# Where the silu gate is multiplied in, and who adds the keys' sums, in a one-core encoder step

## Chip, cores and metric

One Trainium2 chip, one of its cores. The time is that of one execution on the device in microseconds, the median of the runs. The core has TensorE (PE; its weight loads are listed apart as PEld), VectorE (DVE), ScalarE (ACT), GpSimd (POOL) and SyncE (SP), which here only issues DMAs. Each engine works through its own instructions in order; semaphores let one wait for another or for a DMA to land.

## What is computed

One layer of a streaming encoder for 1024 prompt tokens and 64 tokens of a running stream with 512 cached ones, all in fp32. A combined projection feeds two groups of heads; group A is latent attention, group B gated linear attention. What bears on the change:

```python
# group A, keys
kv = (latent @ w_ukv).reshape(B, S, MLA_HEADS, QK_NOPE + V_DIM)
k_nope, v = kv[..., :QK_NOPE], kv[..., QK_NOPE:]
k = jnp.concatenate([k_nope, jnp.broadcast_to(krope[:, :, None, :], ...)], axis=-1)
k = rms_norm(k, g_k_head)            # mean over all 192 columns of a head
# group B, output
o = rms_norm(o, g_gla_out.reshape(GLA_HEADS, GLA_DV))
b_out = o.reshape(B, T, GLA_WIDTH) * jax.nn.silu(r)
# both
x = x + gate1 * (jnp.concatenate([a_out, b_out], axis=-1) @ w_out)
h2 = rms_norm(x, g_norm2) * (1 + scale2) + shift2
x = x + gate2 * (jnp.square(jax.nn.relu(h2 @ w_up)) @ w_down)
```

## The kernel before

A large matmul is made of three fp32r products (high by high, high by low, low by high parts; `mm3`, lines 94 to 96 of the helper). Who makes the parts is `split`: ScalarE copies the high part (line 102), VectorE subtracts (line 103). The work is written as generators, "streams", that a small planner interleaves by estimated times; below that, the framework's scheduler sets each engine's order, except where an instruction is pinned. The order is fixed before the kernel runs: an instruction that waits holds up all behind it on its engine, and SP's queue holds up the DMAs behind it.

The stages the change touches, in order of time:

**Query latents (about 262 to 345 us).** PE makes the latents' rows tile by tile (D1), the columns of the three query groups Q0 to Q2, and the keys and values of the cached tokens. Each latent tile goes PE, ScalarE (square and sum, line 699), GpSimd (`rstd`, lines 121 and 122), VectorE (cn, line 701), PE (transposes of cn, line 715), ScalarE (cl, line 718), then a DMA to lat_d. Beside this `gates()` (line 1371) takes r, the raw gate of group B (128 x 4 heads x 1088 tokens in DRAM, r_d), in four chunks of 272 tokens: load, Silu on ScalarE, store back to r_d. Its tiles live in the pool qp, r with two buffers.

**Keys (`keys_values`, line 986; from 262 to about 456 us).** For each tile of 128 keys, two head pairs each: PE makes k and v in one PSUM bank (g); VectorE copies kn (line 996); ScalarE squares and sums each head (line 998) into ss; VectorE copies v (line 999); GpSimd adds the rotary part's sum ksum and 192 * EPS (line 1000) and takes the power -0.5 (line 1002); VectorE multiplies kn by it (line 1007) and krt (line 1008); PE transposes kn (line 1014) and krt (line 1021). ksum comes from `rotate` (line 966), once for up to four tiles.

**Attention (345 to 545 us), with `out_early` (line 1280) at its end.** While the last attention units run, mh and ml, the parts of mix for the first 272 tokens, are made: group A's heads times rs_d (the softmax sums' reciprocals, broadcast), group B's heads times r, then `split`; PE then does the first four of eight blocks of the projection between the last attention steps.

**Output projection (545 to 640 us, `main` at line 1440).** Four rounds w = 0 to 3 of 272 tokens each. For each later round the half mx[0] (group A) is multiplied by mb (from rs_d), the half mx[1] (group B) by mr (from r_d), both by `gate` (line 1278), then split. Each block of 128 output columns is 24 matmuls; VectorE adds the residual (line 1501), SP stores x2 (line 1503). `load_gates` (line 1452) issues mb (line 1458, one buffer) and mr (line 1459), `load_mix` (1443) mx, `load_x` (1461) the residual. `norm2` follows each round: PE sums squares (line 1523), VectorE (1526) and GpSimd (1527) make the factor st, VectorE a diagonal dg (1530), PE broadcasts it (1534).

Of the kernel before, what the change touches and what calls it, by code (L numbers as in the profile page):

```python
# [10 lines left out]
F32 = mybir.dt.float32  # L11
F32R = mybir.dt.float32r
I32 = mybir.dt.int32
AF = mybir.ActivationFunctionType
ALU = mybir.AluOpType
# [4 lines left out]
P = 128  # L20
# [6 lines left out]
H = 4  # L27
FF = 4096
EPS = 1e-6
# [3 lines left out]
HT = TOK // 2  # L33
# [39 lines left out]
def layer(ctx: ExitStack, tc: tile.TileContext, I, O):  # L73
    nc = tc.nc
    ACT, DVE, POOL, PE, SP = nc.scalar, nc.vector, nc.gpsimd, nc.tensor, nc.sync
# [39 lines left out]
    mhalf = const.tile([P, 4], F32, name="mhalf")  # L115
# [10 lines left out]
    pin = tc.keep_in_program_order  # L126
# [840 lines left out]
    def rotate(k, kn, tab, n):  # L967

        x, cs, sn = kraw[:n, k:k + kn], tabk[:n, tab:tab + kn, 0], tabk[:n, tab:tab + kn, 1]
        a, t = (kw.tile([P, 4, 64], F32, name=name, bufs=1)[:n, 0:kn] for name in ("ra", "rt"))  # L970
        ACT.activation(a, x, AF.Square)
        DVE.reduce_sum(ksum[:n, k:k + kn], a, axis=AX.X)
        DVE.tensor_tensor(out=a, in0=x, in1=cs, op=ALU.mult)
        DVE.tensor_tensor(out=t, in0=x, in1=sn, op=ALU.mult)
        DVE.tensor_tensor(out=x[:, :, 0:32], in0=a[:, :, 0:32], in1=t[:, :, 32:64], op=ALU.subtract)
        DVE.tensor_tensor(out=x[:, :, 32:64], in0=a[:, :, 32:64], in1=t[:, :, 0:32], op=ALU.add)
# [7 lines left out]
    def keys_values(lh, ll, ki, n, kv, slot, ahead=4500):  # L984
        ukh, ukl = groups["UK"]
        kn = kw.tile([P, H, P], F32, name="kn")
        ss = kw.tile([P, 8], F32, name="ssk")

        kr = kw.tile([P, 2, P], F32, name="krt", bufs=1)
        for g in range(2):  # L990
            pk = g_bank()
            for kt in range(2):
                mm3(pk[:n], lh[:, kt, :n], ll[:, kt, :n], ukh[:, kt, 512 * g:512 * g + 512],
                    ukl[:, kt, 512 * g:512 * g + 512], kt == 0, kt == 1)
            pg = pk[:n].rearrange("p (h c) -> p h c", h=2)
            DVE.tensor_copy(kn[:n, 2 * g:2 * g + 2], pg[:, :, 0:P])
            for j in range(2):
                ACT.activation(kr[:n, j], pg[:, j, 0:P], AF.Square, accum_out=ss[:n, 2 * g + j:2 * g + j + 1])
            DVE.tensor_copy(kv.v[:n, slot, 2 * g:2 * g + 2], pg[:, :, P:2 * P])
            POOL.tensor_scalar(out=ss[:n, 4 + 2 * g:6 + 2 * g], in0=ss[:n, 2 * g:2 * g + 2], scalar1=ksum[:n, ki:ki + 1],  # L1000
                               scalar2=192 * EPS, op0=ALU.add, op1=ALU.add)
            POOL.tensor_tensor(out=ss[:n, 4 + 2 * g:6 + 2 * g], in0=ss[:n, 4 + 2 * g:6 + 2 * g], in1=mhalf[:n, 0:2], op=ALU.pow)
            yield 1300, 0, None

        rs = [ss[:n, a:a + 2].rearrange("p (h o) -> p h o", o=1).broadcast_to([n, 2, P]) for a in (4, 6)]
        for g in range(2):
            DVE.tensor_tensor(out=kn[:n, 2 * g:2 * g + 2], in0=kn[:n, 2 * g:2 * g + 2], in1=rs[g], op=ALU.mult)
        DVE.tensor_tensor(out=kr[:n].rearrange("p g (e c) -> p (g e) c", e=2), in0=kraw[:n, ki:ki + 1].broadcast_to([n, H, 64]),
                          in1=ss[:n, 4:8].rearrange("p (h o) -> p h o", o=1).broadcast_to([n, H, 64]), op=ALU.mult)
        cs = slice(P * slot, P * slot + n)  # L1010
        yield 0, ahead, None
        tp = heads(tp_bank())
        for hd in range(H):
            PE.transpose(tp[:, hd, :n], kn[:n, hd], ident[:n, :n])
        ACT.activation(kv.kh[:, :, cs], tp[:, :, :n], AF.Copy, scale=gkhT)
        DVE.scalar_tensor_tensor(out=kv.kl[:, :, cs], in0=tp[:, :, :n], scalar=gkhT, in1=f32(kv.kh[:, :, cs]),
                                 op0=ALU.mult, op1=ALU.subtract)
        yield 450, 800, None
        tp = heads(tp_bank())
        for g in range(2):  # L1020
            PE.transpose(tp[:, g, :n], kr[:n, g], ident[:n, :n])
        for e in range(2):
            hi, lo = slice(64 * e, 64 * e + 64), slice(64 - 64 * e, P - 64 * e)
            ACT.copy(kv.kr[hi, e::2, cs], tp[hi, 0:2, :n])
            DVE.tensor_tensor(out=kv.kr[lo, e::2, cs], in0=tp[hi, 0:2, :n], in1=f32(kv.kr[hi, e::2, cs]), op=ALU.subtract)
        yield 450, 600, None
# [244 lines left out]
    HW = HT // 2  # L1271
# [5 lines left out]
    def gate(t, r):  # L1277
        return DVE.tensor_tensor(out=t, in0=t, in1=r, op=ALU.mult)

    def sums_row(k, kn, t0, n):  # L1280
        return rs_d[k:k + kn, t0:t0 + n].rearrange("(o h) t -> o h t", o=1).broadcast_to([P, kn, n])

    def out_early():
        yield 1000, 0, has("wo 4")
        mixh.append(wctx.enter_context(tc.tile_pool(reuse_waits="tile", name="mixh", bufs=1, side="right")))
        mh, ml = mix_pair()
        b3 = mixh[0].tile([P, 1, HW], F32, name="b3")
        mixh.append((mh, ml))
        def fetch(src, k, kn, t=None):
            t = rawp.tile([P, kn, HW], F32, name="raw") if t is None else t  # L1290
            SP.dma_start(t, sums_row(k, kn, 0, HW) if src is rs_d else src[:, k:k + kn, 0:HW])
            return t

        def halves(k, kn, t):
            split(mh[:, k:k + kn], ml[:, k:k + kn], t, DVE)

        b0, t0, t1 = fetch(rs_d, 0, 3), fetch(mix_d, 0, 3), fetch(mix_d, 4, 2)
        fetch(rs_d, 3, 1, b3)
        yield 0, 5000, None
        pin(gate(t0, b0))  # L1300
        halves(0, 3, t0)
        r1, t3 = fetch(r_d, 0, 2), fetch(mix_d, 3, 1)
        yield 0, 2500, None
        pin(gate(t1, r1))
        halves(4, 2, t1)
        t2, r2 = fetch(mix_d, 6, 2), fetch(r_d, 2, 2)
        pin(gate(t3, b3))
        halves(3, 1, t3)
        yield 0, 3000, None
        pin(gate(t2, r2))  # L1310
        halves(6, 2, t2)
        yield 0, 4250, lambda: not units
        for m in range(4):
            yield 0, 0, lambda: state["banks"] < 4
            state["banks"] += 1
            po = mm_bank()[:, 0:HW]
            for kt in range(KT):
                n, o = wo_place(m, kt)
                mm3(po, wo[n][0][:, o], wo[n][1][:, o], mh[:, kt], ml[:, kt], kt == 0, kt == KT - 1)
                yield 340, 600, None  # L1320
            early.append(po)
# [49 lines left out]
    def gates():  # L1371

        yield 0, 0, has("k 8", "end C1")
        for c in range(4):
            r = qp.tile([P, 4, HT // 2], F32, name="r", bufs=2)
            ts = slice(c * HT // 2, (c + 1) * HT // 2)
            SP.dma_start(r, r_d[:, :, ts])
            yield 0, 3500, None
            ACT.activation(r, r, AF.Silu)
            SP.dma_start(r_d[:, :, ts], r)  # L1380
            yield 0, 1000, None
        tc.keep_in_program_order(ACT.preload_act_table_set("natural_log_exp_and_others"))

# [42 lines left out]
    with ExitStack() as octx:  # L1426
# [11 lines left out]
            return X[10 * (h + 1) + 1 + k // 4][:, k % 4, hs]  # L1438

        def main():  # L1440
            ld = {}

            def load_mix(w):
                if w >= 4:
# [4 lines left out]
                    for _, t0, n, o in place(c)[2]:  # L1449
                        SP.dma_start(ld[c][b][:, :, o:o + n], mix_d[:, 4 * b:4 * b + 4, t0:t0 + n])  # L1450

            def load_gates(w):
                if w >= 4:
                    return
                c = WORDER[w]
                ld[c] += [xw.tile([P, 4, HW], F32, name="mr", bufs=2), xw.tile([P, 4, HW], F32, name="mb", bufs=1)]
                for _, t0, n, o in place(c)[2]:
                    SP.dma_start(ld[c][3][:, :, o:o + n], sums_row(0, H, t0, n))
                    SP.dma_start(ld[c][2][:, :, o:o + n], r_d[:, :, t0:t0 + n])

            def load_x(w):
                if w >= 4:
# [8 lines left out]
            for w, c in enumerate(WORDER):  # L1471
                _, _, parts = place(c)
                if w == 0:
                    mh, ml = mixh[1]
                else:
                    mx = ld.pop(c)
                    mh, ml = mix_pair() if w == 2 else [xw.tile([P, 8, HW], F32R, name=f"m{x}1", bufs=1) for x in "hl"]
                    gate(mx[0], mx[3])
                    split(mh[:, 0:4], ml[:, 0:4], mx[0], DVE)
                    gate(mx[1], mx[2])  # L1480
                    split(mh[:, 4:8], ml[:, 4:8], mx[1], DVE)
                if w == 0:
                    load_x(0)
                    load_mix(1)
                load_gates(w + 1)
                load_x(w + 1)
                load_mix(w + 2)
                acc = last[:, 0:HW] if w == 3 else nw.tile([P, HW], F32, name="acc")
                for m in range(8):
# [586 lines left out]
```

## Time and profile before

| what | value |
|---|---|
| median of 3 runs | 1329.35 us (1327.03 to 1332.3) |
| the profiled execution's own time | 1331.06 us |
| its span, first to last instruction | 1329.2 us |
| granted TensorE clock, mean | 0.999 |
| DMA | 191.40 MB, mean 144 GB/s |

The profile gives each engine's busy time; PE's matmuls are pipelined and their ends modelled, so the number of matmuls in a stretch tells more than its busy share. A row of a timeline has start, duration, engine, line, operation, out<-in, shapes and count; brackets at its end give the idle time of the engine just before and what ended it. A row of the waits has total, times and longest. ACTIVATION_READ_ACCUMULATOR is the second half of an activation that also sums. SPq and ACTq are DMA issues.

### The profile page before, as it was taken

Reading aid. Unit: us, or ns where it says so; the run is one execution under the profiler, and the core shown is the slowest. Engines: PE = TensorE matmul, PEld = TensorE weight load, DVE = VectorE, ACT = ScalarE, POOL = GpSimd, SP = SyncE. Lnnn points to the kernel's source line nnn. Section 1 sums busy time; section 2 is a strip of 40 time slices with the busy share of each in tenths; the row PEclk is TensorE's granted clock in tenths of the full one; section 3 lists DMA queues with packets and bytes.
Section 4 is the critical chain, followed back from the end, with each engine's and each line's share of the span. In section 5 each row is a group of like instructions: output and inputs, shape, how many; then the busy total and the mean of one; then the engine's idle time right before and its main releaser. Section 6 shows DMA issues by size and latency. Waiting matters only on the chain.

```text
span 1329.2 us, 25834 instructions
## 1 busy us (share of the span) xinstructions
PE 1307.7 (98%) x9925; PEld 1248.1 (94%) x9925; DVE 911.7 (69%) x2032; ACT 647.2 (49%) x1608; POOL 77.7 (6%) x136
## 2 busy tenths in 40 slices
PE   9999999999999999999999999999999999999999
PEld 8899999889777889999999999999999999999998
DVE  4898787466577767576999976566546955864554
ACT  5375554564266666443765445444444343333332
POOL 0100010121112200001000000000000000000000
PEclk9999999999999999999999999999999999999999
DMA  9420123384445202792346654344259645442441
GB/s 344 147 75 1 49 77 89 97 238 128 158 131 155 74 16 81 203 283 86 99 150 210 196 172 157 124 158 140 86 206 384 223 160 193 161 127 85 135 127 35
DMA packets 164653, 191.40 MB, mean 144 GB/s; under 512 B 15686, under 2 KB 116914, under 8 KB 164402
## 3 DMA queue, kind: packets, MB, share of 16 engines
q1 hardware_dynamic: 162002, 186.46, 44.3%
q10 hardware_dynamic: 2528, 3.29, 0.7%
q8 instruction: 78, 1.28, 0.4%
q14 instruction: 45, 0.37, 0.1%
HBM read 136.22 MB, written 53.49 MB: 143 GB/s over the span
## 4 chain that ended last, share of the span: by engine, by line
PE 73%; DVE 11%; DMA 7%; ACT 5%; issue 2%; POOL 2%; SPq 0%; ACTq 0%; DVEq 0%; POOLq 0%
PE mm L94 13%; PE mm L96 12%; PE mm L95 12%; PE g L94 5%; PE g L96 5%; PE g L95 5%; PE tp L94 3%; PE tp L96 3%; PE tp L95 3%; PE mm L1094 3%; PE g L1124 2%; PE g L886 1%; PE mm L179 1%; DMA mb<-rs_d 1%; PE tp L1134 1%
## 5 line engine op out<-in xcount | busy, mean ns | idle before, releaser
L102 ACT CAST opers<-quad 128x512 fp32r<-128x512 f32 x112 | 69.5, 621 | 183.3 <-PE mm L96 147.0
L103 DVE TENSOR_TENSOR opers<-quad,opers 128x512 fp32r<-128x512 f32 x112 | 77.3, 690 | 113.7 <-ACT opers L102 113.7
L96 PE MATMUL mm<-opers 128*128 128x272 f32 x448 | 128.7, 288 | 0.0
L94 PE MATMUL mm<-opers 128*128 128x272 f32 x448 | 128.4, 287 | 0.3 <-DVE e L2003 0.3
L95 PE MATMUL mm<-opers 128*128 128x272 f32 x448 | 128.2, 286 | 0.0
L94 PE MATMUL mm<-ah,wh 128*128 128x272 f32 x424 | 121.8, 288 | 0.0
L96 PE MATMUL mm<-ah,wl 128*128 128x272 f32 x424 | 121.8, 288 | 0.0
L95 PE MATMUL mm<-al,wh 128*128 128x272 f32 x424 | 121.7, 287 | 0.0
L94 PE MATMUL mm<-hh,wh 128*128 128x384 f32 (+2 forms) x264 | 90.7, 344 | 0.1
L95 PE MATMUL mm<-hl,wh 128*128 128x384 f32 (+2 forms) x264 | 87.4, 331 | 0.0
L96 PE MATMUL mm<-hh,wl 128*128 128x384 f32 (+2 forms) x264 | 87.0, 330 | 0.0
L94 PEld LDWEIGHTS mm<-opers 128*128 128x128 f32 x448 | 84.5, 189 | 0.5 <-issue 0.5
L96 PEld LDWEIGHTS mm<-opers 128*128 128x128 f32 x448 | 84.2, 188 | 0.0
L95 PEld LDWEIGHTS mm<-opers 128*128 128x128 f32 x448 | 84.1, 188 | 0.0
L94 PEld LDWEIGHTS mm<-ah,wh 128*128 128x128 f32 x424 | 79.9, 188 | 0.0
L95 PEld LDWEIGHTS mm<-al,wh 128*128 128x128 f32 x424 | 79.7, 188 | 0.0
L103 DVE TENSOR_TENSOR opers<-ru,opers 128x544 fp32r<-128x544 f32 x108 | 77.7, 720 | 2.9 <-ACT opers L102 2.7
L96 PEld LDWEIGHTS mm<-ah,wl 128*128 128x128 f32 x424 | 79.6, 188 | 0.1
L102 ACT CAST opers<-ru 128x544 fp32r<-128x544 f32 x108 | 69.6, 645 | 14.0 <-PE mm L96 10.9
L102 ACT CAST wh<-ru 128x512 fp32r<-128x512 f32 x67 | 41.2, 620 | 66.4 <-PE tp L95 21.0
L94 PE MATMUL mm<-wh,hh 128*128 128x264 f32 (+3 forms) x216 | 65.7, 304 | 0.9 <-ACT cl L718 0.9
L96 PE MATMUL g<-opers 128*128 128x272 f32 x224 | 64.7, 289 | 0.0
(415 smaller groups left out, 4228.5 us busy)
## 6 DMA issues: line engine op xcount, KB each, us to landing
ru<-u_d SPq DMA_DIRECT2D x108, 272.0 KB, 2.8
raw<-in_w_ada SPq DMA_DIRECT2D x32, 512.0 KB, 5.3
ru<-in_w_up SPq DMA_DIRECT2D x32, 512.0 KB, 4.2
quad<-in_w_down SPq DMA_DIRECT2D x16, 1024.0 KB, 5.4
u_d<-st SPq DMA_DIRECT2D x60, 272.0 KB, 2.1
u_d<-sc SPq DMA_DIRECT2D x45, 272.0 KB, 2.2
raw<-in_w_in SPq DMA_DIRECT2D x22, 256.0 KB, 6.1
x<-in_xo_T SPq DMA_DIRECT2D x8, 544.0 KB, 7.9
```

Of the source, the lines that this page charges most:

```text
L94: pin(PE.matmul(out, lhsT=ah, rhs=bh, start=first, stop=False, skip_group_check=more))
L95: pin(PE.matmul(out, lhsT=ah, rhs=bl, start=False, stop=False, skip_group_check=more))
L96: pin(PE.matmul(out, lhsT=al, rhs=bh, start=False, stop=last, skip_group_check=more))
L102: ACT.copy(hi, src)
L103: eng.tensor_tensor(out=lo, in0=src, in1=f32(hi), op=ALU.subtract)
L179: mm = PE.matmul(acc[32 * j:32 * j + 32, 0:256], lhsT=scT[:, k, :], rhs=was[k][:, 256 * j:256 * (j + 1)], start=(k == 0), stop=(k == KT - ...
L886: PE.matmul(sc[:n, a, p], lhsT=d[:, w * p + n * a:w * p + n * a + n], rhs=qv[:, :, p, a], start=True, stop=True)
L1094: PE.matmul(sp[:n, :w], lhsT=x[:, hd, :n], rhs=y[:, hd, :w], start=(j == 0), stop=(j == 4))
L1124: PE.matmul(op[:, :n], lhsT=kvs[kt // 4].v[:kw, kt % 4, hd], rhs=pt[:kw, k, :n], start=(kt == 0), stop=(kt == nkt - 1))
L1134: PE.transpose(tp[:kw, k, :n], pr[k0 // 4][:n, P * k:P * k + kw], ident[:n, :n])
```

## The change

Two edits together.

The first multiplies the silu gate into group B's mix already in `gates()`: eight chunks of 136 tokens instead of four of 272; each loads r and its part of mix_d (new tile rm, one buffer), ScalarE takes Silu of r, VectorE multiplies, and the product goes back to mix_d instead of the silu to r_d. So `out_early` and the output projection neither load r nor multiply by it. mr is gone, mb gets three buffers and is issued a round earlier by `load_sums`, ahead of mx.

The second replaces GpSimd's addition of ksum by an Identity activation on ScalarE with ksum as bias, in place in ss; 192 * EPS is added to ksum in `rotate` instead, by VectorE. GpSimd keeps the power.

```diff
 def rotate(k, kn, tab, n):
         DVE.reduce_sum(ksum[:n, k:k + kn], a, axis=AX.X)
+        DVE.tensor_scalar(out=ksum[:n, k:k + kn], in0=ksum[:n, k:k + kn], scalar1=192 * EPS, scalar2=None, op0=ALU.add)
...
 def keys_values(lh, ll, ki, n, kv, slot, ahead=4500):
-            POOL.tensor_scalar(out=ss[:n, 4 + 2 * g:6 + 2 * g], in0=ss[:n, 2 * g:2 * g + 2], scalar1=ksum[:n, ki:ki + 1],
-                               scalar2=192 * EPS, op0=ALU.add, op1=ALU.add)
-            POOL.tensor_tensor(out=ss[:n, 4 + 2 * g:6 + 2 * g], in0=ss[:n, 4 + 2 * g:6 + 2 * g], in1=mhalf[:n, 0:2], op=ALU.pow)
+            ACT.activation(ss[:n, 2 * g:2 * g + 2], ss[:n, 2 * g:2 * g + 2], AF.Identity, bias=ksum[:n, ki:ki + 1])
+            POOL.tensor_tensor(out=ss[:n, 4 + 2 * g:6 + 2 * g], in0=ss[:n, 2 * g:2 * g + 2], in1=mhalf[:n, 0:2], op=ALU.pow)
...
 def out_early():
-        r1, t3 = fetch(r_d, 0, 2), fetch(mix_d, 3, 1)
+        t3 = fetch(mix_d, 3, 1)
         yield 0, 2500, None
-        pin(gate(t1, r1))
         halves(4, 2, t1)
-        t2, r2 = fetch(mix_d, 6, 2), fetch(r_d, 2, 2)
+        t2 = fetch(mix_d, 6, 2)
...
-        pin(gate(t2, r2))
         halves(6, 2, t2)
...
 def gates():
-        for c in range(4):
-            r = qp.tile([P, 4, HT // 2], F32, name="r", bufs=2)
-            ts = slice(c * HT // 2, (c + 1) * HT // 2)
+        for c in range(8):
+            r = qp.tile([P, 4, HT // 4], F32, name="r", bufs=2)
+            ts = slice(c * HT // 4, (c + 1) * HT // 4)
+            m = qp.tile([P, 4, HT // 4], F32, name="rm", bufs=1)
             SP.dma_start(r, r_d[:, :, ts])
-            yield 0, 3500, None
+            SP.dma_start(m, mix_d[:, 4:8, ts])
+            yield 0, 2500, None
             ACT.activation(r, r, AF.Silu)
-            SP.dma_start(r_d[:, :, ts], r)
+            yield 0, 1000, None
+            DVE.tensor_tensor(out=m, in0=m, in1=r, op=ALU.mult)
+            SP.dma_start(mix_d[:, 4:8, ts], m)
             yield 0, 1000, None
...
-            def load_gates(w):
+            def load_sums(w):
...
-                ld[c] += [xw.tile([P, 4, HW], F32, name="mr", bufs=2), xw.tile([P, 4, HW], F32, name="mb", bufs=1)]
+                rows[c] = xw.tile([P, 4, HW], F32, name="mb", bufs=3)
                 for _, t0, n, o in place(c)[2]:
-                    SP.dma_start(ld[c][3][:, :, o:o + n], sums_row(0, H, t0, n))
-                    SP.dma_start(ld[c][2][:, :, o:o + n], r_d[:, :, t0:t0 + n])
+                    SP.dma_start(rows[c][:, :, o:o + n], sums_row(0, H, t0, n))
...
-                    gate(mx[0], mx[3])
+                    gate(mx[0], rows.pop(c))
                     split(mh[:, 0:4], ml[:, 0:4], mx[0], DVE)
-                    gate(mx[1], mx[2])
                     split(mh[:, 4:8], ml[:, 4:8], mx[1], DVE)
                 if w == 0:
                     load_x(0)
+                    load_sums(1)
                     load_mix(1)
-                load_gates(w + 1)
                 load_x(w + 1)
+                load_sums(w + 2)
                 load_mix(w + 2)
```

The scheduler moves other instructions as well. PE's row at the first tile of keys after the query stage (350 us; kn and krt are the keys to be transposed, cqh and cql the query latents' parts, lath and wh the next keys' operands), as a difference:

```order
 L96 MATMUL g<-wh,latl 128x512
 L179 MATMUL mm<-raw,scT 32x256 x4
-L1014 MATMUL tp<-ident,kn 128x128 x2
 L94 MATMUL g<-wh,cqh 64x384
 L95 MATMUL g<-wl,cqh 64x384
@@ -1703,5 +1703,5 @@
 L95 MATMUL g<-wl,cqh 64x384
 L96 MATMUL g<-wh,cql 64x384
-L1014 MATMUL tp<-ident,kn 128x128 x2
+L1014 MATMUL tp<-ident,kn 128x128 x4
 L1021 MATMUL tp<-ident,krt 128x128 x2
 L94 MATMUL g<-wh,lath 128x512
```

The first pair's transposes now stand behind the query matmuls, together with the second pair's. SP's row at the start of the output projection, before (x is the residual, x_d the store of x2, raw here w_out):

```order
L1155 DMA rs_d<-rrow 4x128
L1156 DMA mix_d<-mo 128x4x128
L1246 DMA raw<-in_w_out 128x8x128 x2
L1467 DMA x_6605<-in_xo_T 128x4x272
L1467 DMA x_6606<-in_xo_T 128x4x272
L1450 DMA mx<-mix_d 128x4x208
L1450 DMA mx<-mix_d 128x4x64
L1450 DMA mx<-mix_d 128x4x208
L1450 DMA mx<-mix_d 128x4x64
L1458 DMA mb<-rs_d 128x4x208
L1459 DMA mr<-r_d 128x4x208
```

And the same place now:

```order
L1246 DMA raw<-in_w_out 128x8x128 x3
L1468 DMA x_6643<-in_xo_T 128x4x272
L1155 DMA rs_d<-rrow 4x128
L1156 DMA mix_d<-mo 128x4x128
L1468 DMA x_6644<-in_xo_T 128x4x272
L1504 DMA x_d<-x_6643 128x272
L1460 DMA mb<-rs_d 128x4x208
L1460 DMA mb<-rs_d 128x4x64
L1452 DMA mx<-mix_d 128x4x208
L1452 DMA mx<-mix_d 128x4x64
```

w_out is issued earlier, mb stands ahead of mx and not behind it, and both stand behind the first store of x2, which stood behind all of them before. VectorE's row in the query stage, around 300 us, as it is now (rm is the new product; before, the same rows stood there without the two of L1381):

```order
L1000 COPY v<-g 128x256
L1381 TENSOR_TENSOR rm<-rm,r 128x544
L1007 TENSOR_TENSOR kn<-kn,ssk 128x256
L1008 TENSOR_TENSOR krt<-kraw,ssk 128x256
L701 TENSOR_SCALAR cn<-mm,s_3441 128x256
L705 TENSOR_TENSOR lat<-cn,gkv_bc 128x256
L1363 TENSOR_SCALAR cq<-mm,vT 128x320
L1381 TENSOR_TENSOR rm<-rm,r 128x544
L701 TENSOR_SCALAR cn<-mm,s_3502 128x256
```

Two products, of the fourth and the fifth chunk, now stand in front of a kn and of a cn. Lines of the kernel from 973 on have moved by one or two numbers.

More of the change, by code (lines that the diff above doesn't have):

```diff
@@ L1440, in main @@
         def main():
-            ld = {}
+            ld, rows = {}, {}
             def load_mix(w):
```

## The prediction

> **What bounds the kernel now.** I read the page, then the list of PE's waits, then the stretches of the output projection, then the timelines around each wait that the change can touch.
>
> ```profile
> PE 1307.7 (98%) x9925; PEld 1248.1 (94%) x9925; DVE 911.7 (69%) x2032; ACT 647.2 (49%) x1608; POOL 77.7 (6%) x136
> ```
>
> PE is busy for 1307.7 of 1329.2 us. The change adds and removes no matmul, so it can only fill or open holes in PE's row. The list of PE's waits over the whole span (total, times, longest) names the holes near it:
>
> ```profile
> PE tp L1014 <- DVE kn L1007: 2.3, 4, 1.0
> PE tp L1534 <- DVE dg L1530: 1.4, 1, 1.4
> ...
> PE mm L95 <- DVE ml L103: 1.2, 1, 1.2
> ...
> PE mm L94 <- ACT cl L718: 0.9, 1, 0.9
> ```
>
> Two belong to the keys and the latents (L1014, L718), two to the output projection (L95, L1534). The last two cost more than they say. In four stretches of 10 us of that projection (first PE's busy time and its matmuls, at the end the granted clock, DMA share and GB/s):
>
> ```profile
> 550.00:560.00 10.00, 10.00 (x82) 10.00 (x81) 5.67 (x9) 3.81 (x7) 0.00 (x0) 1.00 1.15 308
> 560.00:570.00 10.00, 8.83 (x70) 8.62 (x69) 7.42 (x12) 3.41 (x5) 0.00 (x0) 1.00 1.13 315
> 570.00:580.00 10.00, 10.00 (x82) 9.96 (x81) 3.77 (x9) 1.30 (x3) 0.00 (x0) 1.00 0.91 232
> 580.00:590.00 10.00, 8.61 (x55) 8.24 (x54) 9.34 (x23) 5.97 (x10) 2.63 (x2) 0.83 1.10 313
> ```
>
> An undisturbed stretch holds 82 matmuls, so one takes 10/82 = 0.122 us. The fourth lacks 27, or 3.3 us, while PE was idle only 1.39 of it: its granted clock was 0.83, and (1 - 0.83) x 10 = 1.7 us went there. The DMA engines are full in most of this stage.
>
> **Output projection: 4.0 us to win.** The waits follow from VectorE, which works in order (start, duration, and in brackets the idle time before):
>
> ```profile
> 555.36 1.32 DVE L1501 SCALAR_TENSOR_TENSOR x<-mm,modT,x 128x272 f32<-128x272 f32 x3 [3.66 <-DMA x<-in_xo_T]
> 564.65 1.29 DVE L1278 TENSOR_TENSOR mx<-mx,mb 128x1088 f32<-128x1088 f32 x1 [1.96 <-DMA mb<-rs_d]
> 567.99 1.28 DVE L103 TENSOR_TENSOR ml<-mx,mh 128x1088 fp32r<-128x1088 f32 x1
> 579.61 1.29 DVE L1278 TENSOR_TENSOR mx<-mx,mb 128x1088 f32<-128x1088 f32 x1 [2.39 <-DMA mb<-rs_d]
> 581.35 0.20 DVE L1526 TENSOR_SCALAR st<-tp 128x2 f32<-128x2 f32 x2
> 583.70 0.77 DVE L1530 TENSOR_SCALAR dg<-ident,st 128x128 f32<-128x128 f32 x3 [0.60 <-POOL st L1527]
> ```
> ```profile
> 578.80 0.63 PE L1523 MATMUL tp<-ones,acc 128*128 128x1 f32 x6
> 584.04 1.03 PE L1534 MATMUL tp<-dg,ones 128*128 128x128 f32 x6 [1.39 <-DVE dg L1530]
> ```
> ```profile
> 581.58 2.63 POOL L1527 TENSOR_TENSOR st<-st,mhalf 128x2 f32<-128x2 f32 x2 [70.36 <-DVE st L1526]
> ```
> ```profile
> 555.51 1.41 SPq L1458 DMA_DIRECT2D mb<-rs_d x1
> 573.08 0.41 SPq L1458 DMA_DIRECT2D mb<-rs_d x1
> ```
>
> The first product waits for mb, which was queued at 555.51 behind mx and only lands for 564.65; the split at 567.99 is what PE wants (1.2 us). The change queues mb ahead of mx, sends no mr, and drops the second product (1.28) between the split's parts. mb now stands behind the first x2 store, which waits for the step that VectorE began at 555.36; that eats the head start, but the second product is gone, and so are the mr of three rounds (3 x 128 x 1088 x 4 bytes, 1.7 MB). I take the whole 1.2 us.
>
> The second chain: PE's sums end at 579.43, but L1526 starts only at 581.35, behind a product that waited 2.39 us for an mb queued at 573.08. With three buffers that mb is loaded a round earlier. L1526 can then start at about 579.5, GpSimd's first power needs 583.70 - 581.58 = 2.1, dg 0.3, so PE could go on at 581.9 to 582.3; it stopped at 584.04 - 1.39 = 582.65. Bounds 0 and 1.4; I take 1.1, since one product and two evictions may still be in front.
>
> The clock: if PE does not stop there, the 1.7 us go too; bounds 0 and 1.7, I take 1.7, because the fall stands right behind this wait. [...]
>
> Nothing of the silu's product is left on VectorE here: 3 x 1.28 us that hid beside matmuls, worth nothing by itself. The two products of the half that is prepared early (128x544) go as well, and the order at the end of the attention shifts: PE now meets the first matmuls of the projection some 3 us earlier, before their mh is surely there. PE was full there; between -0.5 and +1.0 us, taken as 0.
>
> **Keys' sum: 1.3 us to win.** The two GpSimd steps (min/median/max ns), the second pair's product, and the one place where PE waited long:
>
> ```profile
> L1000 POOL TENSOR_SCALAR ssk<-ssk,ksum x26: 292/300/573, 268.2 to 454.7; 128x2 f32<-128x2 f32 x24, 64x2 f32<-64x2 f32 x2
> L1002 POOL TENSOR_TENSOR ssk<-ssk,mhalf x26: 693/708/711, 268.6 to 455.1; 128x2 f32<-128x2 f32 x24, 64x2 f32<-64x2 f32 x2
> ```
> ```profile
> 353.30 0.43 DVE L1007 TENSOR_TENSOR kn<-kn,ssk 128x256 f32<-128x256 f32 x1 [0.76 <-POOL ssk L1002]
> ```
> ```profile
> 350.75 0.44 PE L1014 MATMUL tp<-ident,kn 128*128 128x128 f32 x2 [0.95 <-DVE kn L1007]
> 354.35 0.38 PE L1014 MATMUL tp<-ident,kn 128*128 128x128 f32 x2
> ```
> ```profile
> 297.57 0.27 ACT L998 ACTIVATE krt<-g 128x128 f32<-128x128 f32 x1
> 297.73 0.20 ACT L998 ACTIVATION_READ_ACCUMULATOR krt<-g 128x1 f32 x1
> ```
>
> GpSimd's 0.30 becomes ScalarE's 128x2 step. No row has it; it lies between the 0.20 of a read of one column and the 0.27 of 128 columns, nearer the first, so 0.2: the way to the power is 0.1 us shorter plus one change of engine. [...] The four added EPS sums on VectorE (0.2 each) come long before their use. So 0.1 at each of the three smaller waits: 0.3. The larger gain is in the order: the transposes that waited 0.95 at 350.75 now stand behind the query matmuls with the other two of 354.35, so that wait goes: 1.0. What is late next is the second pair of heads: PE would come to it at 354.35 - 1.3 = 353.0, and its kn was done at 353.7; but its copy now stands ahead of the first pair's product, so that chain starts some 1.5 us earlier (an estimate) and ends at 352.2.
>
> **Query latents' stage: 2.5 us to pay.** The stage takes 8 products, 8 half Silus, 26 sums and 24 transfers of 272 KB instead of 8 of 544 KB: 6.5 MB for 4.4. Prices:
>
> ```profile
> L1278 DVE TENSOR_TENSOR raw<-raw x3: 726/726/1010, 535.2 to 545.2; 128x544 f32<-128x544 f32 x2, 128x816 f32<-128x816 f32 x1
> ```
> ```profile
> L1379 ACT ACTIVATE r<-r x4: 1112/1114/1116, 271.0 to 289.2; 128x1088 f32<-128x1088 f32 x4
> ```
> ```profile
> ru<-u_d SPq DMA_DIRECT2D x108, 272.0 KB, 2.8
> ...
> u_d<-st SPq DMA_DIRECT2D x60, 272.0 KB, 2.1
> ```
> ```profile
> r_d<-r SPq DMA_DIRECT2D x4, 544.0 KB, 4.8
> ```
>
> A product is 0.73, a half Silu about 0.6. rm has one buffer, so a chunk goes round as store (2.1), load (2.8), product (0.73) and some 0.3 of issue: 5.9 us at the quiet prices; with this stage's own 4.8 for a store, up to 10.6 if the load is as slow. Three places have no slack:
>
> ```profile
> 298.18 0.64 ACT L718 ACTIVATE cl<-mm,vT 128x128 f32<-128x128 f32 x2
> ```
> ```profile
> 298.87 0.41 PE L94 MATMUL mm<-wh,hh 128*128 128x320 f32 x1 [0.85 <-ACT cl L718]
> 304.75 0.43 PE L715 MATMUL mm<-ident,cn 128*128 128x128 f32 x2
> 315.56 0.66 PE L1014 MATMUL tp<-ident,kn 128*128 128x128 f32 x4
> ```
> ```profile
> 298.20 0.42 DVE L999 COPY v<-g 128x256 f32<-128x256 f32 x1
> 301.34 0.54 DVE L1365 TENSOR_SCALAR cq<-mm,vT 128x320 f32<-128x320 f32 x1
> 304.20 0.48 DVE L701 TENSOR_SCALAR cn<-mm,s 128x256 f32<-128x256 f32 x1 [2.32 <-POOL s L122]
> 315.30 0.43 DVE L1007 TENSOR_TENSOR kn<-kn,ssk 128x256 f32<-128x256 f32 x1 [0.66 <-POOL ssk L1002]
> ```
>
> First, a Silu and a sum now stand between 297.73 and cl: 0.8 to 0.9 more on a wait that PE already has. Second, one product stands behind L999 (298.6) and the next behind cq (301.9). Between them lie 3.3 us and the round takes 5.9: done at 299.4, stored by 301.5, loaded by 304.4 and with the issue 304.7, multiplied by 305.4. cn starts then and not at 304.20, and PE takes it 0.07 us after its end: 1.2 us late, 0.8 beside the first delay. Third, a product stands between the two copies of kn in front of 315.30: 0.73, and PE has no slack. 0.9 + 0.8 + 0.8 = 2.5. Below: 0, if the 0.66 and 2.32 of idle absorb it. Above: the slow round, below.
>
> SP: the load of rm waits there for the last store, and in front of it queue lat_d, the weights of the third query group and the keys' latr; no wait for any of these stands high among PE's waits now, so I charge nothing.
>
> **Sum.** -1.2 - 1.1 - 1.7 - 1.0 - 0.3 + 2.5 = -2.8 us. The profiled execution took 1331.06, so its like would take 1328.3; the median of the three runs is 1329.35 and gives 1326.5, my forecast.
>
> **Rivals.**
> 1. [...] Chance 0.13.
> 2. SP's queue holds mb and mx behind the x2 store so long that both VectorE waits come back: only 1.3 of the gains are left against 2.5, 1330.5. Against it: that store's data was ready at about 556, nine microseconds before the first product, and 1.7 MB less stands in the queue. Chance 0.12.
> 3. Slower: the round of the one rm buffer. VectorE's places for the eight products spread over some 54 us (272 to 326, an estimate by what stands beside them), 7.7 per round. If store and load take over 3.5 us each the round is longer, every product from the fifth on makes VectorE stand, and cn and kn are late each time. At 10.6 the lag is 3 us a round over four rounds, 12 us in all; with three quarters of it reaching PE, 9 more than the forecast: 1335.5. For it: the 4.8 row comes from this stage. Against: that row moves twice the bytes. Chance 0.13.
> 4. The query stage hides its 2.5 in VectorE's idle time and the remaining 1.3 of kn waits go too: 1322.7. Chance 0.14.
>
> The forecast has 0.48. That the sum doesn't get shorter by ScalarE costs only 0.3 and is no case of its own.
>
> **Range and chances.** About 0.5%, 6.6 us, is what a measurement here can tell from no change; the three runs alone span 5.3. 1321 to 1333 leaves out most of the third rival above and the lower end of the fourth. Faster than 1322.7: most of the fourth and a little of the forecast's spread, 0.12. Slower than 1336: half of the third, 0.08. Same: 0.80.
>
> **What would show it.** Right: no PE wait for ml at 568 nor for dg near 582, about 82 matmuls in each 10 us from 560 to 590 and no clock below 1.00; no kn wait near 350; PE waits grown at cl and new at cn and kn between 298 and 316, 2 to 3 us in sum. Wrong: VectorE standing at L1381 for several us per chunk, or the mb product still waiting for its DMA, or PE waiting for mh at the end of the attention.

## The result, and the profile after

| | before | changed |
|---|---|---|
| median of 5 runs | 1330.53 us (1327.03 to 1332.3) | 1340.28 us (1338.72 to 1341.29) |
| profiled execution: time, span | 1331.06, 1329.2 us | 1341.29, 1339.5 us |
| granted TensorE clock, mean | 0.999 | 0.995 |

The ratio is 1.0072, with a 95% interval of 1.0057 to 1.0088: slower by 9.75 us. The forecast was a gain, with a range up to 1333.

PE's row of the page and its longest waits:

```profile
PE 1311.2 (98%) x9925; PEld 1251.3 (93%) x9925; DVE 912.2 (68%) x2039; ACT 652.3 (49%) x1638; POOL 66.7 (5%) x110
```
```profile
PE tp L1014 <- DVE kn L1007: 4.8, 5, 1.7
PE tp L1535 <- DVE dg L1531: 4.1, 1, 4.1
PE mm L715 <- DVE cn L701: 2.7, 1, 2.7
PE mm L94 <- ACT cl L718: 1.2, 1, 1.2
...
PE mm L94 <- ACT mh L102: 0.9, 1, 0.9
```

The wait for ml is gone from the list, as forecast. The one for dg, which was to go, has tripled, kn's have grown, and a long one for cn has come. Two places carry the loss. The query latents' stage first, of the kernel before (PE's busy time and matmuls, near the end the granted clock):

```profile
300.00:320.00 20.00, 20.00 (x124) 19.18 (x123) 14.78 (x32) 10.91 (x32) 3.43 (x7) 1.00 0.49 133
320.00:340.00 20.00, 19.68 (x115) 17.95 (x115) 8.98 (x24) 4.46 (x17) 2.21 (x4) 1.00 0.24 91
```

The same stretches of the changed kernel:

```profile
300.00:320.00 20.00, 15.94 (x94) 14.55 (x93) 12.34 (x28) 10.74 (x32) 2.32 (x4) 1.00 0.74 195
320.00:340.00 20.00, 16.84 (x90) 15.04 (x89) 11.89 (x26) 7.40 (x22) 1.38 (x2) 0.90 0.54 170
```

In these 40 us PE ran 184 matmuls where it had run 239, at about 0.17 us each (40/239): some 9 us. And the output projection after the change, to be laid beside the four stretches of the prediction:

```profile
560.00:570.00 10.00, 10.00 (x82) 10.00 (x81) 4.88 (x8) 2.74 (x5) 0.00 (x0) 1.00 1.05 241
570.00:580.00 10.00, 10.00 (x81) 10.00 (x81) 7.51 (x12) 3.80 (x7) 0.00 (x0) 1.00 0.93 292
580.00:590.00 10.00, 8.93 (x72) 8.67 (x70) 4.12 (x9) 2.00 (x4) 0.00 (x0) 1.00 1.05 301
590.00:600.00 10.00, 6.96 (x33) 6.70 (x34) 7.62 (x22) 5.25 (x11) 1.24 (x2) 0.66 0.14 47
```

The stretch from 560 to 570 is full now (82 matmuls; it had 70); the last holds 33, at a clock of 0.66.

To divide the whole, I took the starts of the same PE instructions in both traces and their difference (its median per 20 us). It is -1.05 us at 260, before the change does anything; +9.31 at 340; +6.70 at 520; +10.06 at 600. So the query stage lost 10.4 us, the keys won 2.6, and the end of the attention with the projection lost 3.4. The prediction had 2.5 lost, 1.3 won and 4.0 won. All such places are of one traced execution of each kernel. That of before has a fall of the clock at 585.19, to 0.50 for 3.41 us, so some 1.7 us of its projection are the fall's.

**The query stage.** VectorE's eight products start from 271.06 to 333.06, 62.0/7 = 8.9 us apart. Three of them, each with its wait, and the row that PE waited for:

```profile
297.17 0.72 DVE L1381 TENSOR_TENSOR rm<-rm,r 128x544 f32<-128x544 f32 x1 [1.12 <-DMA rm<-mix_d]
...
305.67 0.73 DVE L1381 TENSOR_TENSOR rm<-rm,r 128x544 f32<-128x544 f32 x1 [4.57 <-DMA rm<-mix_d]
306.31 0.48 DVE L701 TENSOR_SCALAR cn<-mm,s 128x256 f32<-128x256 f32 x1
...
333.06 0.72 DVE L1381 TENSOR_TENSOR rm<-rm,r 128x544 f32<-128x544 f32 x1 [1.54 <-DMA rm<-mix_d]
```
```profile
306.84 0.44 PE L715 MATMUL mm<-ident,cn 128*128 128x128 f32 x2 [2.71 <-DVE cn L701]
```

The product stands 4.57 us for rm, cn stands behind it, and PE behind cn. The one rm buffer's round in SP's rows:

```profile
297.93 0.36 SPq L1382 DMA_DIRECT2D mix_d<-rm  x1
298.34 0.53 SPq L1376 DMA_DIRECT2D r<-r_d  x1
...
302.33 0.37 SPq L1377 DMA_DIRECT2D rm<-mix_d  x1
```

Stored at 297.93, loaded again at 302.33, there at 305.67. Each load of rm is issued as the store before it lands. So SP's rows give the stores of all seven rounds: 2.5 us three times and 4.2 to 4.6 four times, 3.6 on average. The loads behind them took 2.9 to 5.1, 3.8 on average, by their last landing in the trace; each is 272 KB. With 0.73 for the product that is 8.1 of the 8.9; in two rounds the product came later still, behind other work of VectorE though rm was there. The r of the next chunk is issued only behind that store too, so ScalarE stands for r as well (at most 3.93 us), and kh, a part of the keys, behind it:

```profile
288.06 0.66 ACT L1379 ACTIVATE r<-r 128x544 f32<-128x544 f32 x1 [3.93 <-DMA r<-r_d]
288.63 0.67 ACT L1015 ACTIVATE kh<-tp,vT 128x512 fp32r<-128x512 f32 x1
```

Over the stage VectorE waited 9.1 us for rm (six times), ScalarE 9.7 for r (five times). The last product, at 333.06, holds up a kn in the same way, and PE stops twice (the second time for 1.46 us):

```profile
334.93 0.31 PE L1014 MATMUL tp<-ident,kn 64*128 64x64 f32 x2 [1.70 <-DVE kn L1007]
```

Of the 10.4 us, 3.4 are the clock: it fell to 0.50 for 6.83 us from 336.09.

**The projection.** SP's rows where the prediction saw the two stops:

```profile
558.39 0.34 SPq L1504 DMA_DIRECT2D x_d<-x  x1
558.82 0.98 SPq L1460 DMA_DIRECT2D mb<-rs_d  x2
559.90 5.29 SPq L1452 DMA_DIRECT2D mx<-mix_d  x4
...
569.87 8.68 SPq L1504 DMA_DIRECT2D x_d<-x  x6
...
581.21 1.63 SPq L1452 DMA_DIRECT2D mx<-mix_d  x2
```

The first load of mx before; VectorE's third product before; VectorE's products now, with the norm's first step:

```profile
550.95 4.46 SPq L1450 DMA_DIRECT2D mx<-mix_d  x4
```
```profile
596.67 1.28 DVE L1278 TENSOR_TENSOR mx<-mx,mb 128x1088 f32<-128x1088 f32 x1
```
```profile
567.91 1.29 DVE L1278 TENSOR_TENSOR mx<-mx,mb 128x1088 f32<-128x1088 f32 x1 [3.69 <-DMA mx<-mix_d]
...
576.50 1.29 DVE L1278 TENSOR_TENSOR mx<-mx,mb 128x1088 f32<-128x1088 f32 x1 [1.23 <-DMA mx<-mix_d]
...
590.00 1.29 DVE L1278 TENSOR_TENSOR mx<-mx,mb 128x1088 f32<-128x1088 f32 x1 [5.32 <-DMA mx<-mix_d]
...
591.75 0.20 DVE L1527 TENSOR_SCALAR st<-tp 128x2 f32<-128x2 f32 x2
```

The loads of mb and mx stand behind the first store of x2. And the third round's product, which before ran behind the whole norm (at 596.67; the norm's step at 581.35), now stands ahead of the norm's first step, L1527, and waits there 5.32 us for its mx, whose load is issued at 581.21, behind six more stores of x2. That is PE's stop of 4.1 us, and the clock falls behind it, from 592.09, to 0.50 for another 6.83 us.

### The profile page after: what moved, and what is told of

The parts are those of the page before. It is cut to its first block, busy times and chain, and to the rows that moved or that the text cites. A ratio compares the mean times of both kernels' runs of the same rounds, so it can differ in the third digit from the quotient of the medians.

```text
span 1339.5 us, 25851 instructions
## 1 busy us (share of the span) xinstructions
PE 1311.2 (98%) x9925; PEld 1251.3 (93%) x9925; DVE 912.2 (68%) x2039; ACT 652.3 (49%) x1638; POOL 66.7 (5%) x110
## 3 DMA queue, kind: packets, MB, share of 16 engines
q8 instruction: 78, 1.28, 0.4%
## 4 chain that ended last, share of the span: by engine, by line
PE 66%; DVE 3%; DMA 2%; ACT 2%; issue 1%; SPq 1%; POOL 0%; DVEq 0%; ACTq 0%
PE mm L94 11%; PE mm L96 11%; PE mm L95 11%; PE g L94 6%; PE g L96 6%; PE g L95 6%; PE tp L94 3%; PE tp L96 3%; PE tp L95 3%; PE mm L1094 2%; PE g L1124 2%; DMA mx<-mix_d 1%; PE mm L179 1%; PE tp L1134 1%; ACT prob L1105 1%
```

## The experiments

My theory after the comparison: three separate things, the round through DRAM in the query stage, a gain at the keys, and the order of SP's loads and VectorE's steps at the projection. The rivals were two: the work itself (VectorE, ScalarE, bytes) has no room in the query stage; or the two edits hurt each other. Each experiment's time stands beside runs of the kernel before made with it (medians 1327.76, 1328.35 and 1327.81 us in the three sets of four, 55 runs in all); the change's stands beside its own five runs of before, median 1330.53. The places are as above, by starts of the same PE instructions against the trace of before (260 to 340, 340 to 520, 520 to 600). Two things must be read along with them. The trace of before carries its own fall of the clock in the projection, so each number in the last column is up to 1.7 us lower than against an execution of before without one; and of the 55 runs of before, 48 show a mean clock of 1.000. And where a kernel's clock fell in the query stage, half the time at a clock of 0.50 is in that column: 3.4 us for the change, 5.1 for e4 and e7, 1.7 for e2, e3, e5, e6 and e9, nothing for the others.

| kernel | us | ratio, 95% interval | query | keys, attention | projection |
|---|---|---|---|---|---|
| the change | 1340.28 | 1.0057 to 1.0088 | +10.4 | -2.6 | +3.4 |
| e1 keys' sum alone | 1322.98 | 0.9953 to 0.9977 | -1.7 | -2.6 | -2.0 |
| e2 product alone | 1341.26 | 1.0087 to 1.0113 | +7.9 | +0.1 | +3.4 |
| e3 change, rm two, r three buffers | 1335.60 | 1.0046 to 1.0070 | +4.7 | -2.6 | +2.3 |
| e4 change, loads pinned | 1333.89 | 1.0033 to 1.0057 | +9.3 | -2.6 | -3.8 |
| e5 e4 without the product | 1330.11 | 1.0006 to 1.0023 | +3.2 | -2.5 | -3.4 |
| e6 e4 without rm's transfers | 1327.69 | 0.9987 to 1.0004 | +3.7 | -2.5 | -3.6 |
| e7 e4, product on GpSimd | 1335.51 | 1.0050 to 1.0075 | +10.6 | -2.5 | -3.2 |
| e8 keys' sum, mb early | 1322.04 | 0.9940 to 0.9965 | -1.5 | -2.5 | -2.7 |
| e9 e3 and e4 together | 1329.10 | 0.9996 to 1.0014 | +4.1 | -2.6 | -0.2 |
| e10 e8 without mr and its products | 1322.85 | 0.9950 to 0.9975 | -1.7 | -2.6 | -2.9 |
| e11 mb early alone | 1326.62 | 0.9983 to 1.0001 | +1.1 | 0.0 | -3.3 |
| e12 e8, first mr early too | 1321.02 | 0.9932 to 0.9957 | -0.9 | -2.6 | -4.7 |

**e1, e2: each edit alone.** e1 is the change without its parts in `gates`, `out_early` and `main`; e2 the change without those in `rotate` and `keys_values`.

> Only ScalarE's sum of the keys (and EPS in the rotation); the gates stay as before. Theory (the loss is all the product's, the sum gains at the keys): 1.5 to 2.5 us faster than before, 1328 to 1329 us; the wait for kn at 350 goes. Rival (the sum is part of the loss, because it queues on ScalarE behind the silus and the casts): between no change and 3 us slower.

> Only the gates' product; the keys' sum stays on GpSimd. Theory (between 262 and 345 us the product loses 10, at the output projection 3): 11 to 13 us slower than before, 1342 to 1343 us. Rival (both edits together make the loss, by ScalarE): at most 8 us slower, under 1339 us.

e1: 4.8 us faster, more than either theory said. e2: 13.5 slower, a little over the theory's 11 to 13. So the product alone makes the loss, and the rival as it stood (at most 8 us) falls. But the edits do touch each other. Together they come to 8.7 us; the change is 9.75 above its own runs of before and 12.5 above e1's and e2's. In the query stage e1 wins 1.7 and e2 loses 7.9, which makes 6.2, and the change lost 10.4. Of the 4.2 between, 1.7 are its longer fall of the clock, and two stops for kn of 0.84 and 0.52 us at 318 to 320, which neither e1 nor e2 has, are another part. Why the keys' sum makes them was not tried.

The keys' 2.6 us belong to the sum alone (e2 and e11 have none of it). The 1.7 that e1 wins in the query stage lie near 300, where before's wait of 0.85 for cl is gone (1.1), and near 330 (0.7); 0.2 are lost at 273. Of before's four waits for kn, those at 350 (0.95) and 408 (0.54) are gone as well, both behind this stage; e1's list has one, at 273:

```profile
PE tp L1014 <- DVE kn L1007: 0.8, 1, 0.8
```

**e3: more buffers.**

```diff
-            r = qp.tile([P, 4, HT // 4], F32, name="r", bufs=2)
+            r = qp.tile([P, 4, HT // 4], F32, name="r", bufs=3)
...
-            m = qp.tile([P, 4, HT // 4], F32, name="rm", bufs=1)
+            m = qp.tile([P, 4, HT // 4], F32, name="rm", bufs=2)
```

> The whole change, with two buffers for rm and three for r in the query latents' stage. Theory (the round store, load, product of the one rm, and r that is loaded behind it, make VectorE and ScalarE stand): of the 10 us lost there 6 to 9 come back, 1331 to 1335 us, no stand of over 2 us at the product's line; the projection's wait for dg near 588 stays. Rival (it is the work itself: eight products, eight silus and 6.5 MB where there is no room): 1338 to 1341 us.

The stage's loss falls from 10.4 to 4.7, so the round made more than half of it (1.7 of the 5.7 are a shorter fall of the clock); but the total stays above the theory's range. With two buffers the scheduler packs the chunks closer, the last product at 304, and one new stop holds what is left. ScalarE's rows and PE's:

```profile
299.32 0.66 ACT L1379 ACTIVATE r<-r 128x544 f32<-128x544 f32 x1 [0.67 <-DMA r<-r_d]
300.00 1.28 ACT L1384 ACT_TABLE_LOAD   x1
301.29 0.38 ACT L699 ACTIVATE cn<-mm 128x256 f32<-128x256 f32 x1
...
301.66 0.62 ACT L718 ACTIVATE cl<-mm,vT 128x128 f32<-128x128 f32 x2
```
```profile
302.33 0.63 PE L94 MATMUL mm<-wh,hh 128*128 128x320 f32 x1 [4.57 <-ACT cl L718]
```

The last Silu waits for its r, the table for the exponential is loaded behind it, and only then come cn's sum and cl. So here a wait for a transfer in ScalarE's row (0.67 us for r, with the table's 1.28 behind it) did the same kind of harm as one in VectorE's. Whether a later table load would help was not tried.

**e4: the projection's loads pinned.** The loads of mb and mx and the stores of x2 are wrapped in `pin`, which keeps them in the order of the code (the loads of x are not, though the expectation names them):

```diff
-                    SP.dma_start(x2_d[:, m, c * HW:(c + 1) * HW], x2)
+                    pin(SP.dma_start(x2_d[:, m, c * HW:(c + 1) * HW], x2))
```

> The whole change, with SP's loads of mb, mx, x and its stores of x2 in the output projection pinned in the order of the code, so that no store stands in front of the first loads of mb and mx. Theory (that store holds the loads back by 5 to 8 us, and the third round's product comes late for the norm's sums): the 3.3 us lost at the projection turn into a gain of 0 to 4, 1333 to 1337 us, VectorE's product near 580 waits under 2 us. Rival (the order at the end of the attention, or the transfers' own time, makes that loss): 1339 to 1341 us.

The projection turns from +3.4 to -3.8 (1.7 of that is before's own fall), the query stage stays (+9.3). The theory holds. VectorE's rows show the order right again, L1527 ahead of the product:

```profile
584.07 0.21 DVE L1527 TENSOR_SCALAR st<-tp 128x2 f32<-128x2 f32 x2 [0.22 <-PE tp L1524]
585.31 1.29 DVE L1278 TENSOR_TENSOR mx<-mx,mb 128x1088 f32<-128x1088 f32 x1 [1.03 <-DMA mx<-mix_d]
```
```profile
580.00:590.00 10.00, 10.00 (x79) 9.64 (x78) 6.33 (x19) 2.25 (x5) 1.21 (x2) 1.00 0.74 218
```

**e5, e6, e7: what in the query stage hurts.** All from e4. e5 leaves out line 1381; e6 has no rm (below); e7 has `POOL.tensor_tensor` for the product.

```diff
-            m = qp.tile([P, 4, HT // 4], F32, name="rm", bufs=1)
...
-            SP.dma_start(m, mix_d[:, 4:8, ts])
...
-            DVE.tensor_tensor(out=m, in0=m, in1=r, op=ALU.mult)
-            SP.dma_start(mix_d[:, 4:8, ts], m)
+            DVE.tensor_tensor(out=r, in0=r, in1=r, op=ALU.mult)
+            SP.dma_start(r_d[:, :, ts], r)
```

> As the one with the pinned loads (1333.9, with 9.3 us lost against before between 260 and 345), but VectorE's eight products in the query latents' stage are left out: r and rm are loaded, silu taken, rm stored back unmultiplied. Transfers, their bytes and ScalarE's silus stay. Theory (VectorE stands at the product for rm's round, and what is behind it comes late): 6 us or more of the 9.3 go, 1325 to 1328 us. Rival (SP's queue, the bytes, or ScalarE standing for r make the loss): under 3 go, 1331 to 1334 us.

> As the one with the pinned loads, but rm is neither loaded nor stored: r is multiplied by itself and goes back to r_d, so mix stays without its gate. VectorE's eight products and ScalarE's silus stay; of the transfers one third, 2.2 MB, and rm's round go, r keeps its two buffers. Theory (rm's round): at most 3 us are lost between 260 and 345, 1325 to 1328 us. Rival (the products and half silus themselves have no room there): over 6 lost, 1331 to 1334 us.

> As the one with the pinned loads, but GpSimd makes the eight products instead of VectorE. Theory (what hurts is that the latents' chain stands behind a product that waits for rm): GpSimd makes the powers of that chain too, so part of the loss stays, 4 to 8 of the 9.3 us, 1329 to 1333 us. Rival (VectorE's own time is short): at most 3 lost, 1325 to 1328 us.

e5: 6.1 of the 9.3 us go in its trace, as the theory says (3.4 of them clock), but its profiled execution (1327.18) was the shortest of eleven; by the medians, each above its own runs of before, it is 4.4 us better than e4 and lies between theory and rival. e6: 3.7 us stay, nearly the theory's 3, and its time is in the theory's range. What stays is one stop again (before's there was 0.85) with a fall of the clock behind it, for a Silu that waited 1.65 us for r in front of cl:

```profile
301.06 0.64 PE L94 MATMUL mm<-wh,hh 128*128 128x320 f32 x1 [3.61 <-ACT cl L718]
```

That stop and the fall make up what is left, so the eight products and eight half Silus cost little besides. e7 fits neither: 10.6 us, all of the loss. A product on GpSimd takes 1.36 us (0.72 on VectorE), GpSimd waits 25.8 us in all for rm (VectorE 8.0 in e4), and cn's powers on GpSimd stand behind it. Taking the products off VectorE thus won nothing here (10.6 us lost, 9.3 in e4) while they wait in the row of another engine of the same chain; the longer product on GpSimd is in this run too and was not taken apart from the wait.

**e8, e11, e12, e10: the projection without the product's move.** In e8, beside the keys' sum, `load_gates` is split; e11 is e8 without the keys' sum; in e12 `load_r(1)` stands ahead of `load_x(1)`; e10 is e8 without mr, its loads and products.

```diff
                 if w == 0:
                     load_x(0)
+                    load_sums(1)
                     load_mix(1)
-                load_gates(w + 1)
                 load_x(w + 1)
+                load_sums(w + 2)
+                load_r(w + 1)
                 load_mix(w + 2)
```

`load_sums` has mb with two buffers, `load_r` mr with one; loads and stores are pinned as in e4.

> The keys' sum by ScalarE, the gates as before (silu in the query stage, product with mr at the projection), and at the projection only the loads moved: mb has two buffers and is loaded a round earlier, ahead of mx, mr has one, and SP's loads and stores there are pinned in the order of the code. Theory (most of the 3.8 us that the pinned change gained at the projection came from the loads' order): 1 to 3 us faster than the keys' sum alone, 1320 to 1322 us. Rival (it came from the products that went): no faster than the keys' sum alone, 1323 to 1326 us.

> Only the projection's loads moved (mb with two buffers a round earlier and ahead of mx, pinned); keys' sum and gates as before. Theory (the stop for dg near 582 and the fall of the clock behind it came from the late mb): 1 to 3 us faster than before, 1325 to 1327 us, no clock under 1 between 560 and 600. Rival (mr, which is late now, takes its place): no change, 1327 to 1329 us.

> The keys' sum with the projection's loads early, and mr's first load moved too, ahead of the second half of x. Theory (the one PE stop left there, 1.7 us for mh behind a product that waits for mr, goes): 1 to 2 us under 1322.0, 1320 to 1321 us. Rival (the stop was hidden by what follows, or x comes late instead): 1321.5 to 1323 us.

> The keys' sum by ScalarE, loads of the projection early and pinned, and no gate's product anywhere: neither in the query latents' stage nor at the projection, where mr isn't loaded either (silu is still made and stored, group B's mix goes on ungated). It shows the most that a free place for the product could bring. Theory (the product at the projection and the load of mr are hidden but for the 1.9 us that mr came late in the run with the early loads): 1319 to 1321 us. Rival (they cost the projection more, as the pinned change's gain of 3.8 suggests): under 1319 us.

e8's time fits the theory, but its gain at the projection (2.7) is little over e1's (2.0), and the intervals of e1 and e8 overlap: not shown by this run. e1's 2.0 lie almost whole between 580 and 592, where before's stop for dg and its fall were. e11 wins 3.3 us in its trace and has a clock of 1.00 throughout; but 3.2 of them lie at that same place, and the 1.4 that it wins at 568 go again at 573, where PE stood 1.17 us for mh behind a product that waited for mr, as the rival says. Its median is 1.2 us lower with an interval that touches 1: unclear by time. In e12, with mr early as well, that stop is gone: 4.7 us are won, the most of all, about 3 without before's fall, and its median is the lowest of these kernels, 6.8 us under before, at the theory's upper end. That is 2.0 more than e1 has, with intervals that just overlap. Its rows show what the prediction wanted from the product's move, without that move:

```profile
560.00:570.00 10.00, 10.00 (x81) 10.00 (x81) 6.68 (x11) 2.97 (x5) 0.00 (x0) 1.00 1.03 323
570.00:580.00 10.00, 10.00 (x81) 9.82 (x79) 7.01 (x20) 3.25 (x9) 1.25 (x2) 1.00 1.01 304
580.00:590.00 10.00, 10.00 (x82) 10.00 (x81) 9.45 (x19) 6.19 (x11) 0.00 (x0) 1.00 0.45 143
```
```profile
573.61 0.21 DVE L1537 TENSOR_SCALAR st<-tp 128x2 f32<-128x2 f32 x2 [0.21 <-PE tp L1534]
```

L1537 is the norm's first step here; it waits for nothing but PE's sums. e10 does no gate product at all and is no faster than e8 or e12 (1322.85; its theory had 1319 to 1321): at the projection the product and mr's load cost nothing that shows once they come in time. It is not quite a bound, for its attention ends otherwise: like every kernel of the table without the product in `out_early` it falls back by 0.6 to 1.1 us between 530 and 550, and those that keep the product there (e1, e8, e11, e12) do not.

**e9: both mendings.** e3's buffers and e4's pins.

> The whole change with both mendings: two buffers for rm and three for r, and the loads of the output projection pinned. Theory (the two losses are separate and the mendings add): 4 to 6 us under the kernel with the buffers alone (1335.6), 1329 to 1332 us. Rival (the pinned loads only gained because the stage before had been late): within 2 us of it, 1333 to 1337.

1329.1 us, at the lower end of the theory: by the medians the two mendings add. The trace, of the slowest of its eleven executions (1331.87), does not show that at the projection (-0.2): there the third product waited 2.93 us for its mx, PE 1.8 for dg, and the clock fell. The whole change, mended twice, is only level with before; in this trace the product's place in the query stage still costs 4.1 us, 1.7 of them clock.

## Why the prediction was wrong, step by step

**Query stage, +2.5 forecast, +10.4 measured: the failed step is the price of the round.** I wrote "5.9 us at the quiet prices" and worked with it ("Between them lie 3.3 us and the round takes 5.9"). The store took 3.6 us on average and up to 4.6, the load 3.8 and up to 5.1, where I had 2.1 and 2.8 from the feed-forward part, and the products came 8.9 apart. The nearest row was this stage's own, 4.8 us for 544 KB; I discounted it because it moves twice the bytes, yet four of seven stores of half the bytes took 4.2 to 4.6. This is the third rival (chance 0.13), whose condition, over 3.5 us per transfer, was just met on average. Its mechanism and its place were right: the fifth product is the one that waited 4.57 us. (The sum also took the third delay, one product of 0.73, as 0.8; that is 0.1 of it.) Two things are in neither account: r's load, which stands behind rm's store in SP's queue and makes ScalarE stand, and 3.4 us of clock.

**ml at 568, -1.2: right.** PE's wait is gone. VectorE still stood there, 3.69 us, for mx and not for mb; the product came early enough all the same.

**dg, -1.1 forecast, +2.7 measured: the failed step is "L1526 can then start at about 579.5".** I took the wait away from the row and did not ask what would stand there in its place. In the new order the scheduler put the next round's product in front of the norm's first step, and that product had an mx to wait for. e4 and e12 show the step right where that order is kept.

**SP, charged nothing: wrong in both places.** In the query stage r's load behind rm's store is SP's order, and ScalarE waited 9.7 us for r. At the projection the sum took mb's head start as lost and no more, though all of mx stands behind the first x2 store too. The second rival (chance 0.12) named that, for 4.0 us above the forecast; of the two waits of VectorE that it feared, the first came back (3.69 us at 568) and did PE no harm, the second shrank (1.23 us at 576.50, from 2.39), and the harm came from a third, 5.32 us at 590. e4 prices this together with the step above: from +3.4 to -3.8.

**Clock, -1.7 forecast, +1.7 measured.** It fell for 6.83 us behind a stop of 4.1 us, where before's fell for 3.41 behind one of 1.4. And most executions did not have the gain to give: of the 55 executions of before that were made beside the experiments, 48 show a mean clock of 1.000. The fall in the profiled one was its own, and taking it off the median was an error of method.

**Keys, -1.3 forecast, -2.6 measured; the step's price wrong.** The wait at 350 went as said, for 1.0 us. ScalarE's step is not 0.2 us:

```profile
L1001 ACT ACTIVATE ssk<-ssk,ksum x26: 275/296/323, 267.0 to 461.8; 128x2 f32<-128x2 f32 x24, 64x2 f32<-64x2 f32 x2
```

It is 0.296, as long as GpSimd's 0.300. Even so the way got shorter by what was forecast: from the end of the second head's sum on ScalarE to the start of the power on GpSimd the median of the 26 is 0.49 us before and 0.41 after, in e1 too. The gain is thus not in the step's duration. Which part of the 4.8 us of e1 comes from the 0.08 and which from the new order was not separated.

**End of the attention, 0 forecast:** PE now waits 0.9 us for mh against 0.2, and the trace falls back by 1.05 us between 530 and 550, at my upper bound of 1.0. As the kernels that keep the product in `out_early` do not, this is a price of the move itself.

The two big misses are 10.4 - 2.5 = 7.9 and 3.4 + 4.0 = 7.4; 1.3 more than forecast came at the keys. That is 14.0 beside the forecast's -2.8, so about +11; the span grew by 10.3. That this closes rests on the one trace of before: against an execution without its fall the loss at the projection would be some 1.7 us more.

## What to carry to other kernels

Work that was hidden beside full matmuls cost nothing that showed (e10, without any gate product, was no faster than e8 or e12); moved to a stage whose small chains PE waits for, it cost what it waited there (that stage lost 10.4 us in the change, 4.1 in e9), so look first for the order or the load that makes it late where it is (e12 won 4.7 us at the projection without the move, where the move was to bring 4.0; 1.7 of both is the fall in the one trace of before). The tile with one buffer that goes load, product, store through DRAM set a beat of its own here (8.9 us, where 5.9 was reckoned): price its round by the transfers of that very stage, and compare it with the spacing of the work. When a load is moved forward, read in the new order what the scheduler puts in the freed place, on the engine that uses the load (here VectorE's product, which waited 5.32 us at 590) and in the queue that issues it (here the stores of x2 ahead of that product's mx).

## What the runs showed of the hardware

In the two traces of before and after, the granted clock fell to 0.50 three times between 260 and 620 us: in before's for 3.41 us at 585.19, in the changed kernel's for 6.83 us at 336.09 and again at 592.09. Each fall has a stop of PE at or just in front of it: before's one of 1.39 us for dg, the changed kernel's first two of 1.70 and 1.46 us for kn, its second one of 4.11 us for dg. But not every stop had a fall behind it: the changed kernel's of 2.71 us at 304.13 had none, and before's of 1.2 us for ml had none. Three stretches, each with the one behind it, of e5, of e2 and of e7 (PE's busy time; the clock is the third number from the end):

```profile
314.29:317.70 3.41, 1.70 (x12) 1.23 (x11) 2.56 (x8) 2.75 (x10) 1.74 (x2) 1.00 0.96 299
317.71:321.11 3.40, 3.40 (x15) 3.36 (x14) 2.84 (x6) 1.40 (x4) 0.00 (x0) 0.50 0.75 185
```
```profile
305.06:308.47 3.41, 1.73 (x11) 1.70 (x12) 2.87 (x6) 1.65 (x5) 0.22 (x1) 1.00 0.37 110
308.48:311.88 3.40, 3.40 (x19) 3.14 (x19) 3.31 (x7) 3.35 (x9) 0.00 (x0) 1.00 0.98 251
```
```profile
297.84:301.25 3.41, 1.76 (x12) 1.44 (x11) 2.98 (x6) 2.13 (x10) 3.24 (x5) 1.00 0.21 62
301.26:304.66 3.40, 3.40 (x25) 3.40 (x24) 1.37 (x3) 0.21 (x1) 0.39 (x1) 1.00 0.83 202
```

PE stood for about half of each first stretch; the clock of the second is 0.50 in e5 and 1.00 in e2 and e7. So a stop cost its own length in these traces, and where the clock fell as well, half the fall's besides: 1.7 us for one of 3.41, 3.4 for one of 6.83. What decides between a fall and none is not shown; no run tried it.
